# Hybrid gated-mixer trunk: v of the attentions stored as [hi, lo] side by side, two products for three, a PSUM bank per group

## The chip, the cores and the metric

The kernel runs on one core of one Trainium2 chip. The metric is the device time of one execution in microseconds, as the median of several runs of the same program. The profile is of one execution, taken by the hardware profiler, with its own time.

## The reference

Two layers run over 256 tokens of width 1024, all in f32. Each has a gated feed-forward block, a mixer with four branches, a cross-attention to 256 memory tokens and a second feed-forward block. The change is in two of the mixer's branches, the attentions (cut):

```python
y_a = conv_module(u_conv, ...)            # 31 taps, 512 channels
y_b = pool_mixer(u_pool, ...)
y_c = nsa_attention(q_n, k_c, v_c, k_s, v_s, k_w, v_w, g_nsa, ...)
y_d = banded_attention(q_s, k_s, v_s, SWA_WINDOW, swa_sinks[l])
merged = sum(gates[:, :, n] * (branches[n] @ w_branch[l, n]) for n in range(4))
x = x + rms_norm(merged @ w_out[l], mix_post_g[l])

# nsa_attention: 8 heads of 64 in 2 groups that share k and v, 256 tokens
o_c = softmax(q k_cmp) @ v_cmp            # compressed keys, 15 blocks
o_s = softmax(q k_sel) @ v_sel            # blocks of 64 chosen by o_c's scores
o_w = softmax(q k_w)  @ v_w               # band of 512
o   = g0 * o_c + g1 * o_s + g2 * o_w      # g: sigmoid gates per head
```

banded_attention is the same for the sliding window of 128 (called swa below), with one more term per head in the softmax's sum.

## The kernel before

Every f32 factor is held as a pair of reduced-precision pieces, hi (ScalarE, ACT, copies and rounds, L266) and lo = value - hi (VectorE, DVE, L269). A product is three matmuls, hi x hi, hi x lo and lo x hi (mm3), all issued from L280 on TensorE (PE). Weights come as 512 KB halves (raw) through SyncE's DMA queue (SP), are split into hi and lo, and used once. The normalised tokens are hTh and hTl, transposed.

PSUM has three pools: mm with two banks (the wide projections), acc with four (scores, values and small projections), tr with two (transposes). A bank holds 128 x 512 f32.

In an attention, the scores of two or four heads go into an acc bank, DVE and ACT make the softmax (pp), PE transposes it (L731, tr<-ident,pp), and pt_split makes pth (ACT) and ptl (DVE), 128x512 each. Then the probabilities are multiplied with v. Output rows are head dimensions, 64 for each of the two groups, columns are heads and tokens. v of group 0 has to go to rows 0 to 63 and that of group 1 to rows 64 to 127, so v is stored with zero columns: vp has, for each half of the keys (kt) and each of three kinds (NSA's selected and window v, swa's v), the columns [v0, 0, 0, v1], once for hi and once for lo. vpg takes [v0, 0] or [0, v1], and the products of both groups add up in one bank per half of the tokens (t). The zero columns are written by ACT at the setup (L404 to L412); put_v fills in v. Each product of vp is pth x hi, pth x lo and ptl x hi.

The compressed part of NSA has its probabilities in pc (DVE, two writes of 128x64 per t), transposed as tr<-ident,pc and multiplied with vc. cmp_value (L1166) adds its product to the same bank as the others and then splits the bank into y (hi by ACT, lo by DVE), which the branch's output projection reads.

nsa (L1095) and swa (L1186) are pipelines of units (t, group, pair of heads), score of one ahead of value of the one before. A scheduler sets the order of the instructions of each engine from the order in the code, from priorities (front() raises one) and from when it expects buffers to be free; the order is then fixed in the program, and each engine works its own off in turn. Beside the attentions run the conv branch's 124 taps per layer on DVE (cy<-t,sp,cy, conv_taps L949), its statistics on PE (acc<-cy,ones, conv_out L962), the projections of the mixer (mm<-hT.., in branch_chunk and gate_chunk, L868 to L896), and swa_proj (L931), which projects swa's q with 48 matmuls of 512 columns into two acc banks (acc<-hi,hTh 128x512 and its two like). The last step of the mixer is the output projection, acc<-hi,y 128x512 first.

Of the kernel before, what the change touches and what calls it, by code (L numbers as in the profile page):

```python
# [7 lines left out]
F32 = mybir.dt.float32  # L8
F32R = mybir.dt.float32r
# [3 lines left out]
ALU = mybir.AluOpType  # L13
AX = mybir.AxisListType

P = 128
# [3 lines left out]
NT = 2  # L20
# [186 lines left out]
class Trunk:  # L207
# [171 lines left out]
    def setup(self):  # L379
        nc = self.nc  # L380
        cst = self.const.tile([P, _NC - P], F32, name="cst")
        nc.sync.dma_start(cst, self.c_d[:, P:])

        def c(nm):
            a, b = _COFF[nm]
            return cst[:, a - P:b - P]

        self.c = c
        idr = self.const.tile([P, P], F32R, name="idr")
        nc.vector.tensor_copy(idr, self.ident)  # L390
        self.idr = idr
        msk = self.const.tile([P, 2, P], F32R, name="msk")
        nc.vector.tensor_copy(msk[:, 0, :], c("swal"))
        nc.vector.tensor_copy(msk[:, 1, :], c("tri"))
        self.mtri4 = msk[:, 1, None, :].to_broadcast([P, 4, P])
        self.mtri2 = msk[:, 1, None, :].to_broadcast([P, 2, P])
        self.mswa = msk[:, None, :, :].to_broadcast([P, 2, 2, P])
        self.cmneg = self.const.tile([P, 2, 16], F32R, name="cmneg")
        self.ts(self.cmneg.rearrange("p a b -> p (a b)"), c("cm"), 1.0, -NEG, ALU.subtract, ALU.mult)
        self.ones = self.const.tile([P, P], F32, name="ones")  # L400
        nc.vector.memset(self.ones, 1.0 / 512)
        self.zero = self.t4([P, 512])
        nc.vector.memset(self.zero, 0.0)
        self.vpad = []  # L404
        for i in range(2):
            row = []
            for kt in range(NT):
                v = self.const.tile([P, 3, 4, 64], F32R, name="vp%d%d" % (i, kt))
                self.act(v.rearrange("p a b c -> p (a b c)")[:, :512], self.zero)
                self.act(v.rearrange("p a b c -> p (a b c)")[:, 512:], self.zero[:, :256])  # L410
                row.append(v)
            self.vpad.append(row)  # L412
        self.vc = []
        for i in range(2):
            v = self.const.tile([P, P], F32R, name="vc%d" % i)
            self.act(v, self.zero[:, :P])
            self.vc.append(v)
        self.kc = self.const.tile([P, 2, 2, 16], F32R, name="kc")
        self.pc = self.const.tile([P, 4, P], F32, name="pc")
        nc.vector.memset(self.pc.rearrange("p a b -> p (a b)"), 0.0)  # L420
# [275 lines left out]

    def put_v(self, kind, t, ps):

        hi, lo = self.vpad[0][t][:, kind, 0::3, :], self.vpad[1][t][:, kind, 0::3, :]
        self.split(hi, lo, ps)  # L700

    def softmax(self, bank, ng, w, wgt=None, nsink=None, on_dve=False):

# [44 lines left out]
            pend = (b, r)  # L748
        pend[0](pend[1])

    def vpg(self, i, kt, kind, g):
        return self.vpad[i][kt][:, kind, 2 * g:2 * g + 2, :].rearrange("p a d -> p (a d)")

    def mixer(self, l, h):
        nc, tc = self.nc, self.tc
# [339 lines left out]
    def nsa(self, qn, kkh, kkl, gt, y, before_cmp):  # L1095
        nc = self.nc
        cm = self.c("cm").rearrange("p (t c) -> p t c", t=2)
        out = [None, None]

        def score(t, g, pr):  # L1100
            h0 = g * 4 + pr * 2
# [19 lines left out]
            return ps  # L1121

        def value(t, g, pr, ps):
            first = out[t] is None
            if first:
                out[t] = self.pacc((P, 4, P))
            dst = out[t][:, 2 * pr:2 * pr + 2, :]
            if t == 0:
                p = self.pt_split([ps[j][:, br, :] for br in range(2) for j in range(2)])
                for br in range(2):  # L1130
                    self.pv(dst, p, slice(2 * br, 2 * br + 2), self.vpg(0, 0, br, g), self.vpg(1, 0, br, g),
                            first and br == 0, False)
                return
            for br in range(2):
                p = self.pt_split([ps[j][:, br, kt * P:(kt + 1) * P] for kt in range(2) for j in range(2)])
                for kt in range(2):
                    self.pv(dst, p, slice(2 * kt, 2 * kt + 2), self.vpg(0, kt, br, g), self.vpg(1, kt, br, g),
                            first and br == 0 and kt == 0, False)

        def cmp_score(t):  # L1140
            if t == 0:
# [24 lines left out]
        def cmp_value(t, _):  # L1166
            tok = slice(t * P, (t + 1) * P)
            p = self.pt_split([self.pc[:, r, :] for r in range(4)])
            self.pv(out[t], p, slice(0, 4), self.vc[0], self.vc[1], False, True)
            self.split(y[0][:, :, tok], y[1][:, :, tok], out[t])  # L1170

        units = [(t, g, pr) for t in range(NT) for g in range(2) for pr in range(2)]
        ready = {}
        for i, u in enumerate(units):
            ready[u] = score(*u)
            if i == 4:
                cmp_score(0)
            if i:
                value(*units[i - 1], ready[units[i - 1]])
            if i == 6:  # L1180
                cmp_value(0, None)
        cmp_score(1)
        value(*units[-1], ready[units[-1]])
        cmp_value(1, None)

    def swa(self, qs, kks, y, mp):  # L1186
        ns = mp.tile([P, 8], F32, name="ns")
        self.ts(ns, self.S_("sinks"), -1.0)
        out = [None, None]

        def score(t, g, pr):
            if t == 0:
                bank = self.pacc((P, 4, P))
                self.matmul(bank, self.idr, self.mtri4, True, False)
                for r in range(4):
                    q = qs[0][:, g * 4 + r, :]
                    self.matmul(bank[:, r, :], q, kks[:, g, 0:P], False, False)
                    self.matmul(bank[:, r, :], q, kks[:, 2 + g, 0:P], False, True)
                return self.softmax(bank, 4, P, None, ns[:, g * 4:g * 4 + 4], True)
            h0 = g * 4 + pr * 2  # L1200
            bank = self.pacc((P, 2, S))
            self.matmul(bank.rearrange("p a (b k) -> p a b k", b=2), self.idr, self.mswa, True, False)
            for j in range(2):
                q = qs[1][:, h0 + j, :]
                self.matmul(bank[:, j, :], q, kks[:, g, :], False, False)
                self.matmul(bank[:, j, :], q, kks[:, 2 + g, :], False, True)
            return self.softmax(bank, 2, S, None, ns[:, h0:h0 + 2], True)

        def value(t, g, pr, p):
            first = out[t] is None  # L1210
            if first:
                out[t] = self.pacc((P, 4, P))
            if t == 0:
                p = self.pt_split([p[:, r, :] for r in range(4)])
                self.pv(out[0], p, slice(0, 4), self.vpg(0, 0, 2, g), self.vpg(1, 0, 2, g), first, g == 1)
            else:
                dst = out[1][:, 2 * pr:2 * pr + 2, :]
                p = self.pt_split([p[:, j, kt * P:(kt + 1) * P] for kt in range(2) for j in range(2)])
                for kt in range(2):
                    self.pv(dst, p, slice(2 * kt, 2 * kt + 2), self.vpg(0, kt, 2, g), self.vpg(1, kt, 2, g),  # L1220
                            first and kt == 0, kt == 1)
            if g == 1 and (t == 0 or pr == 1):
                tok = slice(t * P, (t + 1) * P)
                self.split(y[0][:, :, tok], y[1][:, :, tok], out[t])

        self.pipeline([(lambda t=t, g=g, pr=pr: score(t, g, pr), lambda p, t=t, g=g, pr=pr: value(t, g, pr, p))
                       for t in range(NT) for g in range(2) for pr in range(1 + t)])

# [134 lines left out]
```

## Time and profile before

| | us |
|---|---|
| median of 3 runs | 1590.31 (1589.11 to 1591.09) |
| profiled execution | 1588.27 |
| its span in the trace | 1586.5 |
| PE busy | 1561.8 |
| DVE busy | 1148.1 |
| ACT busy | 860.8 |
| granted clock of PE, mean | 0.999 |

The page gives busy time per engine over the span. PE's matmuls overlap, so the sum of the durations is more than the span they take, and their start-to-start distance is what one costs. 285.57 MB come in by DMA at 180 GB/s on average. The rows of the trace give the start of an instruction from the span's start, its duration, engine, line, operation, and output and inputs with their shape. A row with x2 or x4 holds that many matmuls.

### The profile page before, as it was taken

The page shows a single profiled execution, that of the slowest core. Times are in us where ns is not written, and L with a number is a line of the kernel's source. Part 1 is how long each engine was busy: PE and PEld are TensorE (multiplying, and loading weights), DVE is VectorE, ACT ScalarE, POOL GpSimd, SP SyncE. Part 2 cuts the span into 40 slices and gives each one's busy share as a digit, 9 for nine tenths or more (in the row PEclk, how much of TensorE's full clock was granted, in tenths as well). Part 3 has the DMA queues.
Part 4 walks back from the last instruction along what each step waited for, and adds up shares of the span by engine and source line. Part 5 has one row for each costly group of instructions (what it writes and reads, how often), then busy time and mean ns, then how long its engine had stood idle before and what let it go on. Part 6 is the DMA issues. An engine that isn't in the chain of part 4 may idle for free.

```text
span 1586.5 us, 28413 instructions
## 1 busy us (share of the span) xinstructions
PE 1561.8 (98%) x11324; PEld 1468.4 (93%) x11324; DVE 1148.1 (72%) x1875; ACT 860.8 (54%) x1461; POOL 21.6 (1%) x44
## 2 busy tenths in 40 slices
PE   6999999999999999999999999999999999999998
PEld 6999889999998988999899987999999999899986
DVE  6666579999878576666566656799998785676653
ACT  6445455675656464545444544656755564554442
POOL 0000000000000000000000000000000000000000
PEclk9999999999999999999999999999999999999999
DMA  7555646644455554555655566465435565445562
GB/s 256 179 188 179 231 152 208 214 134 133 154 173 196 187 184 152 180 191 177 230 172 190 189 198 208 143 227 177 146 121 167 176 206 183 160 164 187 188 201 99
DMA packets 79909, 285.57 MB, mean 180 GB/s; under 512 B 8992, under 2 KB 9760, under 8 KB 79776
## 3 DMA queue, kind: packets, MB, share of 16 engines
q1 hardware_dynamic: 79776, 283.75, 54.0%
q8 instruction: 89, 1.46, 0.4%
q14 instruction: 44, 0.36, 0.1%
HBM read 282.67 MB, written 1.05 MB: 179 GB/s over the span
## 4 chain that ended last, share of the span: by engine, by line
PE 89%; DMA 4%; DVE 3%; ACT 2%; issue 1%; SPq 0%; DVEq 0%; POOLq 0%; ACTq 0%
PE mm L280 55%; PE acc L280 32%; DMA raw<-in_stream_dram 3%; ACT hi L266 1%; DVE lo L269 1%; PE tr L474 1%; PE tr L731 1%; DMA x<-in_x_dram 1%; DVE cy L277 0%; PE tr L280 0%; ACT yw L266 0%; DVE yw L269 0%; PE tr L693 0%; ACT t L266 0%; PE tr L632 0%
## 5 line engine op out<-in xcount | busy, mean ns | idle before, releaser
L269 DVE TENSOR_TENSOR lo<-raw,hi 128x1024 fp32r<-128x1024 f32 (+1 forms) x468 | 565.8, 1215 | 259.6 <-ACT hi L266 255.2
L266 ACT ACTIVATE hi<-raw 128x1024 fp32r<-128x1024 f32 (+1 forms) x468 | 489.6, 1054 | 347.6 <-PE mm L280 211.0
L280 PE MATMUL mm<-hTh,lo 128*128 128x256 f32 x2048 | 575.2, 281 | 0.0
L280 PE MATMUL mm<-hTl,hi 128*128 128x256 f32 x2048 | 573.8, 280 | 0.0
L280 PE MATMUL mm<-hTh,hi 128*128 128x256 f32 x2048 | 573.1, 280 | 0.5 <-ACT hi L266 0.5
L280 PEld LDWEIGHTS mm<-hTh,hi 128*128 128x128 f32 x2048 | 385.1, 188 | 1.1 <-ACT hi L266 0.9
L280 PEld LDWEIGHTS mm<-hTh,lo 128*128 128x128 f32 x2048 | 384.9, 188 | 0.6
L280 PEld LDWEIGHTS mm<-hTl,hi 128*128 128x128 f32 x2048 | 384.9, 188 | 0.3
L280 PE MATMUL acc<-hi,mid 128*128 128x512 f32 x512 | 156.9, 390 | 0.5 <-ACT hi L266 0.5
L280 PEld LDWEIGHTS acc<-hi,mid 128*128 128x128 f32 x512 | 96.0, 188 | 21.3 <-ACT hi L266 1.6
L277 DVE SCALAR_TENSOR_TENSOR cy<-t,sp,cy 128x256 f32<-128x256 f32 x240 | 107.9, 480 | 0.0
L266 ACT ACTIVATE mid<-t 128x256 fp32r<-128x256 f32 x76 | 31.8, 419 | 137.4 <-DVE t L277 137.4
L280 PE MATMUL acc<-lo,mid 128*128 128x512 f32 x256 | 98.0, 390 | 0.1
L280 PE MATMUL mm<-y,hi 128*128 128x256 f32 x512 | 94.1, 282 | 0.0
L280 PE MATMUL acc<-hi,hTh 128*128 128x256 f32 (+2 forms) x272 | 87.6, 323 | 1.5 <-ACT hTh L266 1.4
L280 PE MATMUL acc<-hi,hTl 128*128 128x256 f32 (+2 forms) x272 | 87.6, 322 | 1.2 <-DVE hTl L269 1.2
L280 PE MATMUL acc<-lo,hTh 128*128 128x256 f32 (+2 forms) x272 | 87.4, 322 | 0.0
L280 PEld LDWEIGHTS mm<-y,hi 128*128 128x128 f32 x512 | 79.5, 188 | 1.0
L280 PE MATMUL mm<-y,lo 128*128 128x256 f32 x256 | 72.6, 284 | 0.0
L277 DVE SCALAR_TENSOR_TENSOR t<-t,mm 128x256 f32<-128x256 f32 x160 | 66.8, 417 | 2.6
L269 DVE TENSOR_TENSOR mid<-t,mid 128x256 fp32r<-128x256 f32 x76 | 32.4, 426 | 36.9 <-ACT mid L266 36.9
L280 PEld LDWEIGHTS acc<-lo,mid 128*128 128x128 f32 x256 | 48.1, 188 | 10.8 <-DVE lo L269 1.0
(248 smaller groups left out, 2240.1 us busy)
## 6 DMA issues: line engine op xcount, KB each, us to landing
raw<-in_stream_dram SPq DMA_DIRECT2D x508, 512.0 KB, 4.4
g<-in_gains_dram SPq DMA_DIRECT2D x18, 512.0 KB, 3.8
raw<-in_stream_dram SPq DMA_DIRECT2D x8, 280.0 KB, 3.2
t<-in_mem_dram SPq DMA_DIRECT2D x4, 512.0 KB, 4.0
out_dram<-x SPq DMA_DIRECT2D x4, 256.0 KB, 2.0
x<-in_x_dram SPq DMA_DIRECT2D x2, 256.0 KB, 3.1
x<-in_x_dram SPq DMA_DIRECT2D x1, 512.0 KB, 9.3
t<-in_small_dram SPq DMA_DIRECT2D x2, 256.0 KB, 5.2
```

Source lines behind the costliest of these rows:

```text
L266: return self.nc.scalar.activation(out, in_, func, **kw)
L269: return self.nc.vector.tensor_tensor(out, a, b, op=op)
L277: return self.nc.vector.scalar_tensor_tensor(out, a, s, b, op0=op0, op1=op1)
L280: return self.nc.tensor.matmul(out, lhsT, rhs, start=start, stop=stop, skip_group_check=True)
L474: tr = self.nc.tensor.transpose(pt[:, j, :], xn[:, j * P:(j + 1) * P], self.ident)
L731: self.nc.tensor.transpose(pt[:, j, :], s_, self.ident)
```

## The change

v is stored once per half of the keys, without zeros, as [hi0, lo0, lo1, hi1] of 64 columns each for the two groups (vhl). vpg takes [hi0, lo0] or [lo1, hi1]. pv2 then multiplies that with pth and with ptl, two matmuls in place of three; the output rows are now one group's product with hi in one half and with lo in the other. (The product of ptl with lo, which mm3 leaves out, comes with it.) So the two groups no longer share a bank: each (t, group) gets a bank of acc. fold brings the halves together when a group is done: ACT copies the half with lo from the bank to yf in SBUF, shifted to the group's rows, and DVE adds the half with hi, 64x512 each, both with a raised priority. NSA's compressed product goes to an acc bank of its own, and DVE adds it to yf, 128x512. y is split from yf. In all, a layer has eight folds. The eight zero writes of the setup are gone. The compressed product itself still has three matmuls. The scheduler sets the order of all instructions anew.

```diff
-        self.vpad = []
-        for i in range(2):
-            row = []
-            for kt in range(NT):
-                v = self.const.tile([P, 3, 4, 64], F32R, name="vp%d%d" % (i, kt))
-                self.act(v.rearrange("p a b c -> p (a b c)")[:, :512], self.zero)
-                self.act(v.rearrange("p a b c -> p (a b c)")[:, 512:], self.zero[:, :256])
-                row.append(v)
-            self.vpad.append(row)
+        self.vhl = [self.const.tile([P, 3, 4, 64], F32R, name="vp%d" % kt) for kt in range(NT)]
...
-        hi, lo = self.vpad[0][t][:, kind, 0::3, :], self.vpad[1][t][:, kind, 0::3, :]
-        self.split(hi, lo, ps)
+        self.split(self.vhl[t][:, kind, 0::3, :], self.vhl[t][:, kind, 1:3, :], ps)
...
+    def vpg(self, kt, kind, g):
+        return self.vhl[kt][:, kind, 2 * g:2 * g + 2, :].rearrange("p a d -> p (a d)")
+    def pv2(self, out, p, n, v, start, stop):
+        self.matmul(out, v, p[0][:, n, :], start, False)
+        self.matmul(out, v, p[1][:, n, :], False, stop)
+    def fold(self, yf, bank, g):
+        a, b = slice(g * 64, g * 64 + 64), slice(64 - g * 64, 128 - g * 64)
+        with self.front():
+            self.act(yf[a], bank[b])
+            self.tt(yf[a], yf[a], bank[a], ALU.add)
...
         def value(t, g, pr, ps):                      # nsa
-            first = out[t] is None
+            first = pr == 0
             if first:
-                out[t] = self.pacc((P, 4, P))
-            dst = out[t][:, 2 * pr:2 * pr + 2, :]
+                bank[0] = self.pacc((P, 4, P))
+                if g == 0:
+                    out[t] = self.ap.tile([P, 4, P], F32, tag="yf", bufs=2, name="yf")
+            dst = bank[0][:, 2 * pr:2 * pr + 2, :]
...
+            if pr == 1:
+                self.fold(out[t], bank[0], g)
...
         def cmp_value(t, _):
...
-            self.pv(out[t], p, slice(0, 4), self.vc[0], self.vc[1], False, True)
-            self.split(y[0][:, :, tok], y[1][:, :, tok], out[t])
+            cmp = self.pacc((P, 4, P))
+            self.pv(cmp, p, slice(0, 4), self.vc[0], self.vc[1], True, True)
+            with self.front():
+                self.tt(out[t], out[t], cmp, ALU.add)
+                self.split(y[0][:, :, tok], y[1][:, :, tok], out[t])
```

swa's value is changed in the same way as nsa's.

The first place is PE at the end of NSA in layer 1. In the order of before, the 48 projection matmuls for swa's q (hi, lo with hTh, hTl, 128x512) stand between the products of the probabilities (pth, ptl with vp and vc) and the transposes of pp:

```order
L280 MATMUL acc<-hi,hTh 128x512
L280 MATMUL acc<-lo,hTh 128x512
L280 MATMUL acc<-hi,hTl 128x512
L280 MATMUL acc<-hi,hTh 128x512
L280 MATMUL acc<-lo,hTh 128x512
L280 MATMUL acc<-hi,hTl 128x512
L280 MATMUL acc<-pth,vc_214 128x512
L280 MATMUL acc<-pth,vp_202 128x256
L280 MATMUL acc<-ptl,vc_214 128x512
L280 MATMUL acc<-pth,vc_216 128x512
L731 MATMUL tr<-ident,pp 128x128 x4
L280 MATMUL acc<-ptl,vp_202 128x256
```

In the order of after the same stretch has transposes and products alone, and the projection begins behind the last compressed product and four conv statistics:

```order
L280 MATMUL acc<-ptl,vp_202 128x256
L280 MATMUL acc<-pth,vp_203 128x256
L280 MATMUL acc<-ptl,vp_203 128x256
L280 MATMUL acc<-pth,vp_202 128x256
L722 MATMUL tr<-ident,pc 128x128 x4
L280 MATMUL acc<-ptl,vp_202 128x256
L280 MATMUL acc<-pth,vp_203 128x256
L280 MATMUL acc<-ptl,vp_203 128x256
L280 MATMUL acc<-pth,vc_204 128x512
L280 MATMUL acc<-cy,ones 128x256 x4
L280 MATMUL acc<-hi,hTh 128x512
L280 MATMUL acc<-lo,hTh 128x512
```

All 48 projection matmuls moved from ahead of the last tr<-ident,pc to behind it, and three of the conv statistics with them.

The second place is DVE at the same end of NSA, around its last write of pc (s_.. are columns of softmax sums and gates, t_.. the compressed scores, cy the conv taps). In the order of before:

```order
L269 TENSOR_TENSOR ptl<-tr,pth 128x512
L277 SCALAR_TENSOR_TENSOR cy<-t_2789,sp,cy 128x256 x2
L269 TENSOR_TENSOR s_3762<-s_3762,gt_2618 128x8
L269 TENSOR_TENSOR lo<-raw,hi 128x1024
L277 SCALAR_TENSOR_TENSOR cy<-t_2789,sp,cy 128x256
L269 TENSOR_TENSOR pc<-t_3759,s_3762 128x4x16 x2
L269 TENSOR_TENSOR lo<-raw,hi 128x1024
L277 SCALAR_TENSOR_TENSOR cy<-t_2789,sp,cy 128x256
L269 TENSOR_TENSOR lo<-raw,hi 128x1024 x2
L269 TENSOR_TENSOR ptl<-tr,pth 128x512
```

In the order of after:

```order
L269 TENSOR_TENSOR t_3741<-t_3741,cst 128x128
L1163 TENSOR_REDUCE s_3743<-t_3741 128x8
L273 TENSOR_SCALAR s_3743<-s_3743 128x8
L1165 RECIPROCAL s_3744<-s_3743 128x8
L269 TENSOR_TENSOR s_3744<-s_3744,gt_2608 128x8
L269 TENSOR_TENSOR pc<-t_3741,s_3744 128x4x16 x2
L269 TENSOR_TENSOR ptl<-tr,pth 128x512 x3
L269 TENSOR_TENSOR yf<-yf,acc 64x512
L269 TENSOR_TENSOR cy<-cy,acc 128x1024
L269 TENSOR_TENSOR yf<-yf,acc 128x512
L269 TENSOR_TENSOR y<-yf,y 128x4x128
L269 TENSOR_TENSOR lo<-raw,hi 128x1024 x2
```

Before, a weight split (lo) and taps stand just ahead of pc and splits behind it. After, the last ptl's and the yf adds stand right behind pc, and no tap or split stands in the rows ahead of it.

## Rows read from the trace of the kernel before

**Rows 1.** The page: busy us (share) per engine.
```profile
PE 1561.8 (98%) x11324; PEld 1468.4 (93%) x11324; DVE 1148.1 (72%) x1875; ACT 860.8 (54%) x1461; POOL 21.6 (1%) x44
```

**Rows 2.** Timeline of PE (start, us, instruction) and groups of 371.4 to 390.
```profile
371.25 0.28 PE L280 MATMUL mm<-hTh,lo 128*128 128x256 f32 x1
371.37 0.59 PE L280 MATMUL acc<-cy,ones 128*128 128x256 f32 x2
...
372.03 0.40 PE L280 MATMUL acc<-lo,hTh 128*128 128x512 f32 x1
372.26 0.39 PE L280 MATMUL acc<-hi,hTl 128*128 128x512 f32 x1
...
L280 PE MATMUL acc<-hi,hTh 128*128 128x512 f32 x16 | 6.6, 413 | 0.0
```

**Rows 3.** Windows: busy us of PE, PEld, DVE, ACT, POOL; clock, DMA share, GB/s.
```profile
237.00:290.00 53.00, 51.37 (x434) 50.62 (x433) 50.81 (x108) 30.56 (x47) 0.00 (x0) 1.00 0.65 214
290.00:340.00 50.00, 49.77 (x413) 48.77 (x412) 49.41 (x111) 34.70 (x91) 0.00 (x0) 1.00 0.53 175
340.00:386.00 46.00, 46.00 (x338) 43.31 (x337) 42.78 (x101) 29.08 (x61) 0.00 (x0) 1.00 0.35 117
```

**Rows 4.** Timeline of PE and DVE about the last pc, and PE's output projection.
```profile
385.41 0.36 DVE L269 TENSOR_TENSOR pc<-t,s 128x64 f32<-128x64 f32 x2
...
388.52 0.60 PE L280 MATMUL acc<-cy,ones 128*128 128x256 f32 x2
388.95 0.60 PE L731 MATMUL tr<-ident,pc 128*128 128x128 f32 x4
...
479.56 0.86 PE L280 MATMUL acc<-hi,y 128*128 128x512 f32 x3
```

**Rows 5.** Groups of the whole span, shapes apart: products of probabilities with v.
```profile
L280 PE MATMUL acc<-pth,vp 128*128 128x256 f32 x128 | 28.8, 285 | 0.0
...
L280 PE MATMUL acc<-ptl,vp 128*128 128x256 f32 x64 | 18.3, 286 | 0.2
```

**Rows 6.** DVE groups of 237 to 386 (busy, mean ns, idle before); two timeline rows.
```profile
L269 DVE TENSOR_TENSOR lo<-raw,hi 128x1024 fp32r<-128x1024 f32 x48 | 58.4, 1220 | 2.5 <-ACT hi L266 2.5
...
L269 DVE TENSOR_TENSOR ptl<-tr,pth 128x512 fp32r<-128x512 f32 x12 | 8.1, 678 | 1.6 <-ACT pth L266 1.6
...
381.72 0.68 DVE L269 TENSOR_TENSOR ptl<-tr,pth 128x512 fp32r<-128x512 f32 x1
382.32 0.19 DVE L1159 RECIPROCAL s<-s 128x8 f32<-128x8 f32 x1
```

**Rows 7.** Groups, shapes apart: the nearest DVE and ACT instructions to the new ones.
```profile
L269 DVE TENSOR_TENSOR t<-t,sp 64x240 f32<-64x240 f32 x8 | 4.3, 575 | 1.2 <-ACT t L266 1.2
...
L269 DVE TENSOR_TENSOR y<-acc,y 128x512 fp32r<-128x512 f32 x8 | 5.5, 690 | 3.6 <-ACT y L266 3.6
...
L266 ACT ACTIVATE y<-acc 128x512 fp32r<-128x512 f32 x8 | 4.7, 591 | 10.6 <-PE acc L280 10.6
...
L269 DVE TENSOR_TENSOR vp<-acc,vp 128x128 fp32r<-128x128 f32 x12 | 3.2, 282 | 0.1
```

**Rows 8.** The start: ACT and PE timeline; the load of x from the chain.
```profile
2.01 3.41 ACT L266 ACTIVATE vp<-t 128x512 fp32r<-128x512 f32 x8
...
3.52 9.29 DMA x<-in_x_dram
...
14.10 0.58 PE L280 MATMUL acc<-hi,hTh 128*128 128x256 f32 x1 [1.37 <-ACT hTh L266]
...
17.77 0.41 PE L280 MATMUL acc<-hi,hTh 128*128 128x256 f32 x1
17.98 0.32 PE L280 MATMUL acc<-lo,hTh 128*128 128x256 f32 x1
```

**Rows 9.** Timeline of PE in layer 2, the same two matmuls.
```profile
1170.61 0.60 PE L731 MATMUL tr<-ident,pc 128*128 128x128 f32 x4
...
1261.15 0.86 PE L280 MATMUL acc<-hi,y 128*128 128x512 f32 x3
```

More of the change, by code (lines that the diff above doesn't have):

```diff
@@ L749, in pipeline @@
         pend[0](pend[1])
-    def vpg(self, i, kt, kind, g):
-        return self.vpad[i][kt][:, kind, 2 * g:2 * g + 2, :].rearrange("p a d -> p (a d)")
+    def vpg(self, kt, kind, g):
[8 more added lines that the diff above has]
+            self.tt(yf[a], yf[a], bank[a], ALU.add)
     def mixer(self, l, h):
@@ L1097, in nsa @@
         cm = self.c("cm").rearrange("p (t c) -> p t c", t=2)
-        out = [None, None]
+        out, bank = [None, None], [None]
         def score(t, g, pr):
@@ L1130, in value @@
                 for br in range(2):
[L1131 to L1138, printed above, removed]
+                    self.pv2(dst, p, slice(2 * br, 2 * br + 2), self.vpg(0, br, g), first and br == 0, br == 1)
+            else:
+                for br in range(2):
+                    p = self.pt_split([ps[j][:, br, kt * P:(kt + 1) * P] for kt in range(2) for j in range(2)])
+                    for kt in range(2):
+                        self.pv2(dst, p, slice(2 * kt, 2 * kt + 2), self.vpg(kt, br, g),
+                                 first and br == 0 and kt == 0, br == 1 and kt == 1)
+            if pr == 1:
+                self.fold(out[t], bank[0], g)
         def cmp_score(t):
@@ L1188, in swa @@
         self.ts(ns, self.S_("sinks"), -1.0)
-        out = [None, None]
+        out, bank = [None, None], [None]
         def score(t, g, pr):
@@ L1209, in value @@
         def value(t, g, pr, p):
-            first = out[t] is None
-            if first:
-                out[t] = self.pacc((P, 4, P))
+            if pr == 0:
+                bank[0] = self.pacc((P, 4, P))
+                if g == 0:
+                    out[t] = mp.tile([P, 4, P], F32, tag="yf", bufs=2, name="yf")
             if t == 0:
                 p = self.pt_split([p[:, r, :] for r in range(4)])
-                self.pv(out[0], p, slice(0, 4), self.vpg(0, 0, 2, g), self.vpg(1, 0, 2, g), first, g == 1)
+                self.pv2(bank[0], p, slice(0, 4), self.vpg(0, 2, g), True, True)
             else:
-                dst = out[1][:, 2 * pr:2 * pr + 2, :]
+                dst = bank[0][:, 2 * pr:2 * pr + 2, :]
                 p = self.pt_split([p[:, j, kt * P:(kt + 1) * P] for kt in range(2) for j in range(2)])
                 for kt in range(2):
[L1220 to L1224, printed above, removed]
+                    self.pv2(dst, p, slice(2 * kt, 2 * kt + 2), self.vpg(kt, 2, g), pr == 0 and kt == 0, kt == 1)
+            if t == 0 or pr == 1:
+                self.fold(out[t], bank[0], g)
+                if g == 1:
+                    tok = slice(t * P, (t + 1) * P)
+                    self.split(y[0][:, :, tok], y[1][:, :, tok], out[t])
         self.pipeline([(lambda t=t, g=g, pr=pr: score(t, g, pr), lambda p, t=t, g=g, pr=pr: value(t, g, pr, p))
```

## The prediction

> **What bounds the kernel now.** I read the busy times of the page first, then the stretch that the change touches, by windows and by timelines. TensorE (PE) is busy for 1561.8 of 1586.5 us, 98% [rows 1]. So nearly every matmul stands in the end time at its start-to-start pace, not at the longer duration that a row shows, because matmuls overlap: 0.12 us for 256 columns, 0.23 us for 512, 0.43 us for a conv statistic (cy against ones) or four transposes [rows 2, 4]. The first look therefore says that fewer matmuls give a shorter kernel.
>
> The second look goes to the stretch. The attention over NSA's heads lies at 237 to about 390 us in layer 1, and there VectorE (DVE) is nearly as full as PE: 50.81 of 53, 49.41 of 50 and 42.78 of 46 us, 6.0 us idle in 149 [rows 3]. It works off splits of weights, 58.4 us of them [rows 6], and conv taps between the attention's own steps. At the end of the stretch PE stays full, 46.00 of 46 [rows 3], only because it has something else to do: from about 372 on it runs 48 matmuls of 512 columns that project q for the sliding-window attention (acc from hi and lo weights and hT), 48 x 0.23 = 10.9 us, in between the attention's tail [rows 2] (there is the row of one of the three kinds, 16 each). They need nothing from DVE and hold two of the four acc banks. Behind them come the last transposes of the compressed probabilities (pc) at 388.95, for which DVE wrote pc at 385.41, and from there to the first matmul of the output projection, at 479.56, PE runs without a break: 90.6 us [rows 4]. Layer 2 has the same distance, 1170.61 to 1261.15 [rows 9].
>
> **Removed.** Each product of probabilities with v has two matmuls in place of three: in both layers together 192 of 256 columns become 128 [rows 5], and by the order 12 of 512 become 8. 64 x 0.117 + 4 x 0.23 = 8.4 us, 4.2 a layer, of which 2.8 lie in NSA and 1.4 in the sliding-window attention.
>
> At the start ACT's eight zero writes go, 3.41 us from 2.01 [rows 8]. ACT is free at 5.42 in before, but a piece of x that the chain waits for lands only at 3.52 + 9.29 = 12.81 [rows 8]. That DMA hides most of it; what may be left is the work that ACT does behind 5.42 for the first pieces of x. I put it between 0 and 2 us and take -0.5, near the hidden end, since the load was issued long before ACT was free and lands 7 us after.
>
> **Added off PE.** Per layer: eight ACT copies and eight DVE adds of 64x512 (fold), and two DVE adds of 128x512 for the compressed part. The nearest DVE row is 128x512 out of PSUM, 0.69 us long [rows 7], and 0.60 from start to start for one of that size [rows 6]. Half the partitions should save nothing where the time goes by columns, but no row of before has 64x512. The only row on 64 partitions is 64x240 at 0.575, which would make 1.2 us of 512 columns; the smallest PSUM row, 128x128 at 0.282, is the other end [rows 7]. I take 0.60, from the row with the same columns. ACT's copies are like y from acc, 0.591 [rows 7], and ACT has room (29.08 of 46 [rows 3]), so they cost nothing but delay. Of the DVE adds four stand ahead of the last pc in the order of after; one tap more stands there too (0.39), one weight split less (1.13), one ptl less (0.60). Sum on DVE up to pc: 2.4 + 0.39 - 1.13 - 0.60 = +1.0 us.
>
> **Moved, and this decides.** A bank per (t, group) in place of one per t, and one more for the compressed part, means that scores, two value banks and the compressed sum can hold all four acc banks in NSA's tail. In the order of after the 48 projection matmuls no longer stand in the tail; all of them come after the last pc transposes. PE then has only the tail's own work, about 9 us of transposes and products, for a stretch that DVE sets, and cannot reach ahead. What DVE sets hardly moves, so the 10.9 us of filler that were free in before become time behind the meeting point.
>
> Worked out from the last pc transposes to the first matmul of the output projection: +48 x 0.227 = 10.9 for the projection; three more conv statistics behind the point, 3 x 0.43 = 1.3; eleven products of 256 and two of 512 fewer, -1.3 and -0.45. 90.6 + 10.45 = 101.0 us, as long as PE is full there, which the rows of before show (it had no gap in 90.6 us, and DVE has the most to do early in it).
>
> When do the transposes start? By the count on DVE, pc is written at 385.41 + 1.0 = 386.4 if the 6.0 us idle up to there stay. In PE's order four products stand ahead of the transposes whose ptl DVE makes right behind pc, so the transposes come 0.36 + 0.68 and a few products later, about 388.1: 0.85 earlier than 388.95, since no projection stands in PE's queue any more. The last rows of DVE before pc are the attention's own chain alone, with no tap or split; if what DVE waited for there comes sooner, because PE is free, pc may be ready at 384.1, and the point 3 us earlier. That second value is my estimate from the durations of the chain's steps. I take 1.65 earlier, nearer the count. Per layer: 10.45 - 1.65 = +8.8 us. Two layers have the same order: 17.6 - 0.5 at the start = **+17 us**. The 8.4 us removed are in this sum where they can show: of NSA's 2.8 a layer most lie ahead of the point, in PE time that now waits for DVE anyway, and are worth nothing there.
>
> The profiled execution has 1588.27 us (span 1586.5, 1.8 around it), so 1605.3 by this; the median is 1590.31, 2.0 above the profiled one, which gives **1607**. For the ends: with all of DVE's idle time gone (6 us earlier, less its 1.0 of new work), 5.45 a layer, minus 2 at the start, +8.9; with adds at 0.3 us another 1.2 a layer less, which ends at 1596.8. With adds at 1.2 us DVE is 2.4 later a layer, and with no idle time regained 10.45 + 1.0 + 2.4 = 13.9, times two: 1618.
>
> **Rivals.** A: the order, as above. B, on the other side: the saved matmuls count at face value, -8.4 - 0.5, so 1581 to 1582. For it: PE's 98% [rows 1]. Against it: the point from which it decides. The pc transposes must start at 388.95 - 10.45 = 378.5 for a layer to lose nothing, and 4.2 us before that for face value. So pc must be ready 8 to 12 us before 386.4, while DVE had 6.0 us idle up to there, and its idle time is put to ACT's hi and pth, 2.5 and 1.6 [rows 6], not to matmuls that go away. It holds only if DVE's order of after brings pc forward past taps and splits by more than I counted.
>
> C: the clock. At the start, after PE had been idle, matmuls of 256 columns begin 0.21 apart up to 17.98 [rows 8], later 0.12 apart [rows 2], where the granted clock reads 1.00 [rows 3]: the lower and the upper of the levels 1.2 and 2.4 GHz. In before the tail has no gap. In after PE waits some 8 us of the tail in pieces of a few us. If the clock falls there and has to climb as at the start (17 matmuls from 14.10 to 17.98, each 0.095 too long), that is 1.6 us a layer, +3.2: 1610. The pieces are short and matmuls stand between them, so I hold it for the less likely.
>
> The Trainium skill, "TensorE: Matmul & The Clock Gate", section "Why this matters for your kernels", wants no idle gaps between matmul bursts, because a clock that has fallen must climb again. By that rule, rival C holds in both layers; no gap of before's tail shows it.
>
> D: half of B. pc comes forward by 8 to 9 us a layer, the moved projection is paid for, and nothing is left of the gain: 1587 to 1593. A bank that comes free early on the chip cannot bring it about, since each engine works its instructions off in the order printed above. That the products aren't removed can be left out: the order has 68 matmuls fewer.
>
> **How the numbers follow.** A has 0.70, C 0.18 (inside A's range, above its middle), B 0.08, D 0.04. The likeliest is A: 1607. The range 1596 to 1618 holds A with its unknown prices and C; B and D, 0.12 together, stay out. Faster by over 0.2% (3.2 us, about what a measurement of this kernel can tell from no change) is B, 0.08; within it D, 0.04; slower A and C, 0.88.
>
> **What would show it.** In after, in layer 1: the last projection tile of the mixer before the tail ends near 364, and from there to the pc transposes PE is idle for some 8 to 16 us, with DVE near full up to its last taps. From the pc transposes to the first output-projection matmul it is about 101 us, in both layers. The yf adds last about 0.7, the copies 0.6 or less. The granted clock in the tail tells A from C. I am wrong if PE stays above 95% in the tail, or if that distance is 90 us, or if the pc transposes come before 380.

## The result and the profile after

The changed kernel takes 1608.24 us (median of 4, 1607.96 to 1608.85) against 1589.73 us for the kernel before, run beside it on the same chip: a ratio of 1.0121, 95% interval 1.0108 to 1.0133, or 18.5 us slower by the medians (19.2 by the ratio). The forecast was 1607, with 1596 to 1618 as its range.

The page of the changed kernel, with the same columns as [rows 1], shows nothing at first sight: PE is as busy as before, with 68 matmuls fewer.

```profile
PE 1568.9 (98%) x11256; PEld 1469.8 (92%) x11256; DVE 1162.0 (72%) x1895; ACT 866.8 (54%) x1469; POOL 21.5 (1%) x44
```

The windows of the stretch do (start:end and length, then busy us of PE, PEld, DVE, ACT and POOL, granted clock, DMA share, GB/s). Up to 364 us PE is as full as in [rows 3]. Then comes NSA's tail:

```profile
340.00:364.00 24.00, 23.79 (x197) 23.21 (x195) 23.91 (x54) 16.44 (x34) 0.00 (x0) 1.00 0.47 152
364.00:386.00 22.00, 15.45 (x71) 12.53 (x72) 19.40 (x55) 14.04 (x39) 0.00 (x0) 0.72 0.14 48
...
368.00:377.00 9.00, 6.99 (x25) 5.94 (x26) 9.00 (x28) 4.10 (x11) 0.00 (x0) 0.50 0.09 34
377.00:383.00 6.00, 4.43 (x30) 3.38 (x28) 5.27 (x19) 5.34 (x17) 0.00 (x0) 1.00 0.01 3
383.00:389.00 6.00, 5.46 (x22) 4.68 (x23) 2.80 (x6) 1.77 (x4) 0.00 (x0) 0.72 0.00 0
```

From 364 to 386 us PE is busy 15.45 of 22 us and works part of that at the lower clock level: 0.50 from 368 to 377 is 1.2 of 2.4 GHz. It goes back to 1.00 and falls once more. Shorter windows put the first fall between 366 and 367, and show PE busy without a break ahead of the rise:

```profile
365.00:366.00 1.00, 0.71 (x6) 0.62 (x6) 1.00 (x3) 1.00 (x5) 0.00 (x0) 1.00 0.66 242
366.00:367.00 1.00, 0.23 (x3) 0.00 (x0) 1.00 (x5) 1.00 (x6) 0.00 (x0) 0.85 0.69 234
367.00:368.00 1.00, 0.58 (x1) 0.29 (x1) 1.00 (x3) 1.00 (x5) 0.00 (x0) 0.50 0.72 246
372.00:377.00 5.00, 5.00 (x18) 4.21 (x19) 5.00 (x12) 1.29 (x4) 0.00 (x0) 0.51 0.00 0
```

The weight stream stands still behind it (48 GB/s, then nothing). PE's timeline (start, us, instruction, idle before and what ended it) shows what it waits for:

```profile
363.52 0.27 PE L722 MATMUL tr<-ident,pp 128*128 128x128 f32 x1
365.29 0.94 PE L722 MATMUL tr<-ident,pp 128*128 128x128 f32 x6 [1.50 <-ACT pp L266]
367.09 0.58 PE L280 MATMUL acc<-pth,vp 128*128 128x256 f32 x1 [0.85 <-ACT pth L266]
368.12 0.58 PE L280 MATMUL acc<-ptl,vp 128*128 128x256 f32 x1 [0.45 <-DVE ptl L269]
...
371.87 1.08 PE L722 MATMUL tr<-ident,pc 128*128 128x128 f32 x4 [1.89 <-DVE pc L269]
...
374.23 0.41 PE L280 MATMUL acc<-msk,idr 128*128 128x256 f32 x1
...
375.30 0.41 PE L280 MATMUL acc<-msk,idr 128*128 128x256 f32 x1
...
384.90 1.05 PE L722 MATMUL tr<-ident,pc 128*128 128x128 f32 x4
...
388.75 0.58 PE L280 MATMUL acc<-hi,hTh 128*128 128x512 f32 x1
...
487.74 1.09 PE L280 MATMUL acc<-hi,y 128*128 128x512 f32 x4
```

Every step of the attention's chain is there bare: softmax (pp), transposes, pth, ptl, products, and no other matmul in between. The two scores of the last unit (acc<-msk,idr begins a score) come only at 374.23 and 375.30. In the kernel before they came at 353.50 and 359.92, with the last pc transposes at 388.95 [rows 4]:

```profile
353.50 0.29 PE L280 MATMUL acc<-msk,idr 128*128 128x256 f32 x1
...
359.92 0.28 PE L280 MATMUL acc<-msk,idr 128*128 128x256 f32 x1
```

In the changed kernel, at 388.75 the projection begins, behind everything, and at 487.74 the output projection. Layer 2 is the same (1176.61 and 1279.38).

### The profile page after: what moved, and what is told of

It reads as the page before. It is cut to its first block, busy times and chain, and to the rows that moved or that the text cites. A ratio compares the mean times of both kernels' runs of the same rounds, so it can differ in the third digit from the quotient of the medians.

```text
span 1606.1 us, 28314 instructions
## 1 busy us (share of the span) xinstructions
PE 1568.9 (98%) x11256; PEld 1469.8 (92%) x11256; DVE 1162.0 (72%) x1895; ACT 866.8 (54%) x1469; POOL 21.5 (1%) x44
## 4 chain that ended last, share of the span: by engine, by line
PE 87%; DMA 4%; DVE 3%; ACT 3%; issue 1%; SPq 0%; POOL 0%; DVEq 0%; POOLq 0%; ACTq 0%
PE mm L280 52%; PE acc L280 33%; DMA raw<-in_stream_dram 4%; ACT hi L266 1%; DVE lo L269 1%; PE tr L722 1%; PE tr L466 1%; DVE cy L277 1%; DMA t<-in_mem_dram 1%; ACT pp L266 0%; PE tr L280 0%; ACT yw L266 0%; ACT t L266 0%; PE tr L685 0%; DVE ptl L269 0%
## 5 line engine op out<-in xcount | busy, mean ns | idle before, releaser
L280 PEld LDWEIGHTS acc<-hi,hTl 128*128 128x128 f32 x272 | 52.3, 192 | 6.2 <-DVE hTl L269 2.8
```

The costliest lines, as they stand in the source:

```text
L280: return self.nc.tensor.matmul(out, lhsT, rhs, start=start, stop=stop, skip_group_check=True)
```

## The experiments

The comparisons below are all with the kernel before on the same chip. In the table, layer 1 is cut at three points: the first matmul of the pool branch's gate projection (236.01 in before), the last pc transposes, and the output projection's first matmul.

| kernel | median, us | ratio (95%) | first cut | cut 1 to pc | pc to output projection |
|---|---|---|---|---|---|
| before | 1587.9 to 1589.7 | 1 | 236.01 | 152.94 | 90.61 |
| changed | 1608.24 | 1.0121 (1.0108, 1.0133) | 234.10 | 150.80 | 102.84 |
| own bank alone | 1614.59 | 1.0158 (1.0139, 1.0177) | 235.95 | 152.93 | 102.65 |
| two products alone | 1584.24 | 0.9971 (0.9959, 0.9984) | 236.21 | 151.79 | 89.40 |
| NSA alone | 1610.30 | 1.0137 (1.0119, 1.0155) | 233.12 | 150.54 | 103.02 |
| sliding window alone | 1596.29 | 1.0045 (1.0030, 1.0059) | 235.36 | 152.96 | 94.92 |
| the same, no folds | 1585.95 | 0.9983 (0.9973, 0.9993) | 234.29 | 152.60 | 89.12 |
| the same, direct | 1595.04 | 1.0043 (1.0030, 1.0055) | 235.53 | 152.64 | 94.20 |
| changed, q in mm | 1611.28 | 1.0136 (1.0117, 1.0154) | 233.85 | 158.02 | 95.88 |
| before, q in mm | 1597.81 | 1.0058 (1.0044, 1.0072) | 235.88 | 156.78 | 90.46 |
| changed, two in tr | 1619.72 | 1.0196 (1.0180, 1.0211) | 233.28 | 163.26 | 95.58 |
| the same, direct | 1612.92 | 1.0153 (1.0137, 1.0170) | 234.47 | 164.03 | 96.87 |

**The bank alone.** The compressed product gets its own bank in the kernel before, with an ACT copy and a DVE add of 128x512 to join it:

```diff
-            self.pv(out[t], p, slice(0, 4), self.vc[0], self.vc[1], False, True)
+            cmp = self.pacc((P, 4, P))
+            self.pv(cmp, p, slice(0, 4), self.vc[0], self.vc[1], True, True)
+            self.act(yf, out[t]); self.tt(yf, yf, cmp, ALU.add)   # then y from yf
```

> The kernel before with three products per value and padded v, but with the compressed product of NSA in an acc bank of its own: ACT copies the value bank to SBUF and DVE adds the compressed bank, one each of 128x512 per half of the tokens. Nothing is saved on TensorE, no fold is added. In its order all 48 projection matmuls stand behind the last pc transposes, as in the changed kernel, with 100.3 us of matmul work from there to the output projection where before has 88.8. Theory (bank and order): +9 to +10 us a layer as in the changed kernel (10.2 measured there), 1607 to 1611. Rival (the folds' own work on DVE and ACT is what costs): nearly nothing of the folds is here, so within 3 us of before.

It is 25.1 us slower by its ratio, more than the theory said and far from the rival. Its timeline of PE has the picture of the changed kernel, without any of its folds or its two-product form:

```profile
373.62 0.28 PE L280 MATMUL acc<-msk,idr 128*128 128x256 f32 x1
374.20 0.28 PE L280 MATMUL acc<-msk,idr 128*128 128x256 f32 x1
377.82 0.39 PE L280 MATMUL acc<-cmneg,idr 128*128 128x256 f32 x1 [0.53 <-ACT pp L266]
382.48 0.88 PE L731 MATMUL tr<-ident,pp 128*128 128x128 f32 x2 [2.79 <-ACT pp L266]
383.86 1.54 PE L731 MATMUL tr<-ident,pp 128*128 128x128 f32 x6 [0.51 <-ACT pp L266]
386.36 0.58 PE L280 MATMUL acc<-ptl,vp 128*128 128x256 f32 x1 [0.32 <-DVE ptl L269]
388.87 0.57 PE L731 MATMUL tr<-ident,pc 128*128 128x128 f32 x3
...
491.52 0.86 PE L280 MATMUL acc<-hi,y 128*128 128x512 f32 x3
```

The last scores come 14 to 20 us later than in before, and the last pc transposes at the same time (152.93 after the first cut, 152.94 before). So one more acc bank held, with a copy and an add per half of the tokens, is enough for the whole damage: the scores don't run ahead, the projection doesn't come in, PE stands, and what it could have done waits behind pc. The same copy and add without the bank wasn't run, so the bank's share is not told apart from theirs and from the new order that the scheduler makes for any edit.

**NSA alone, sliding window alone.** In each run one attention has the change and the other its form of before.

```diff
# NSA alone: v of kinds 0 and 1 as [hi0, lo0, lo1, hi1], pv2, fold and cmp bank in nsa; swa as before
# sliding window alone: kind 2 so, pv2 and fold in swa; nsa as before, one yf buffer
```

> The change in NSA alone; the sliding-window attention keeps its padded v and three products. Its order has all 48 projection matmuls behind the last pc transposes. Theory (order): the whole loss of the changed kernel stays and the 2.8 us saved in the sliding-window attention are missing, so 18.5 + 2.8, 1608 to 1612. Rival (the loss is spread over both attentions by their folds): about half of the changed kernel's loss, 1598 to 1600.

> The change in the sliding-window attention alone; NSA and its banks as before. In its order the projection stays in NSA's tail. Theory (order): 8 products of 256 and 2 of 512 columns fewer a layer, 1.4 us each, so -2.8, and about -1 at the start for zero writes that fall away: 1585 to 1588. Rival (folds cost): four folds a layer stay, so slower than before by 3 us or more.

NSA alone is 21.8 us slower by its ratio, as expected: the whole loss is there. The sliding window alone was expected to gain and loses 7.1, so there the rival held. PE's timeline, ACT's copy of the last half and the DVE add, all of layer 1:

```profile
472.82 1.31 PE L280 MATMUL mm<-y,hi 128*128 128x256 f32 x3 [3.75 <-ACT y L266]
...
469.33 0.59 ACT L266 ACTIVATE yf<-acc 64x512 f32<-64x512 f32 x1
...
471.42 0.69 DVE L269 TENSOR_TENSOR yf<-yf,acc 64x512 f32<-64x512 f32 x1
```

PE waits 3.75 us for y at the end of this attention, where in before the first such matmul came at 470.16 without a wait, and the clock falls (0.81 from 468 to 477). The row of before:

```profile
470.16 0.40 PE L280 MATMUL mm<-y,hi 128*128 128x256 f32 x2
```

**Without folds, and with a shorter chain.** Twice more the sliding window alone. First y comes right from each bank's half with hi:

```diff
-                self.fold(out[t], bank[0], g)
-                if g == 1: self.split(y[0][:, :, tok], y[1][:, :, tok], out[t])
+                self.split(y[0][a, :, tok], y[1][a, :, tok], bank[0][a])
```

> The change in the sliding-window attention alone, without folds: y is split right from each bank's half with hi, 64x512, so the half with lo is left out of the result. Same matmuls as in the run with the change in this attention alone, which was 7.4 us slower than before with a stall of 4 us of TensorE at the end of this attention, a layer. If the folds cause that stall (copy, add, then split, two more steps ahead of the branch's first matmul), it goes, and the saved matmuls show: -2.8 and -0.7 at the start, 1585 to 1587. If the stall comes from the new order of the matmuls, it stays: 1593 to 1597.

It gains 2.7 by its ratio, and pc to output projection is 1.49 us shorter, as the 1.4 saved in this attention predict. In the direct form y hi is copied at once, and only y lo takes in the other half:

```diff
+                    self.act(y[0][a, :, tok], bank[0][a])
+                    self.act(yf[a], bank[0][b])
+                    self.tt(yf[a], yf[a], y[0][a, :, tok], ALU.subtract)
+                    self.tt(y[1][a, :, tok], yf[a], bank[0][a], ALU.add)
```

> The change in the sliding-window attention alone, with y hi copied right from the bank's half and the half with lo added to y lo; the result is complete. Theory: as without folds (-3.2 us measured there): 1584 to 1587.5, a version ahead of both kernels. Rival (two more DVE and ACT instructions per group, whatever they wait for, cost as the folds did): 1592 or more.

That missed: 6.8 slower. The chain from the last product to y hi is as short as in before, and still the branch waits. The last products themselves come late, at 468.08, where without folds they come at 463.24 (1.3 us of that is there already at the pc transposes). From 455 to 468 PE has no wait. It has done the other projections by the last products, where without folds it has 3.4 us of matmuls left between them and y. Then it waits 1.29 us for y from ACT, 0.85 for a gate and 0.47 for DVE's y. That the units are later because the folds' instructions stand in the queues of ACT and DVE among the softmax, pth and ptl is a reading of the order; no run here shows it.

**The projection moved back.** swa's q projection goes to the two mm banks, in the changed kernel and, as a control, in the kernel before:

```diff
-        acc = self.tok_major("qs", h, 512)
+        acc = self.tok_major("qs", h, 512, 2, self.pmm)
```

> The changed kernel with one edit: the projection of the sliding-window q writes to the two mm banks in place of two acc banks, so NSA's banks can't keep it out. In its order all 48 projection matmuls stand in NSA's tail again, ahead of the last pc transposes; from there to the output projection are 88.3 us of matmul work (changed kernel 99.2). Theory (bank and order): the tail is filled, the clock stays up, and the loss of 10 to 12 us a layer is gone: 1582 to 1590. Rival (folds and the longer chain cost in themselves): at least half of the loss stays, 1598 or more.

> The kernel before with the same edit, the projection into the mm banks; all else as before. Control for the last one. Theory: TensorE had no idle time in the tail of the kernel before, so there is nothing to gain from a free bank: within 4 us of before, 1586 to 1593. If acc banks were short in the kernel before as well, it gains 4 us or more.

Both missed, and the first has the time of its rival. The projection is back in the tail of the changed kernel, from 363.56 to 375.65, and pc to output projection shrinks from 102.84 to 95.88. But the last pc transposes come 7.2 us later. PE fills the tail with the projection and then waits for the same bare chain, which starts later:

```profile
363.56 0.40 PE L280 MATMUL mm<-hi,hTh 128*128 128x512 f32 x1
375.65 0.39 PE L280 MATMUL mm<-hi,hTl 128*128 128x512 f32 x1
...
379.57 0.28 PE L280 MATMUL acc<-msk,idr 128*128 128x256 f32 x1
...
387.54 2.54 PE L722 MATMUL tr<-ident,pp 128*128 128x128 f32 x8 [2.24 <-ACT pp L266]
```

The last unit's scores begin at 379.57 now, 5.3 us later than in the changed kernel. So to put the displaced projection back does not take the loss away. What this leaves is the reading that the scores have to run ahead, which the next runs try, and the rival, the folds' own cost, which has the bank alone against it: that kernel has none of the folds and loses more. The control is 9.2 us slower than before, with pc 3.8 us later, so this edit is not free itself; against it the change costs 13.5 us (1611.28 to 1597.81).

**Two banks from tr.** The compressed scores and product go to the tr pool, which leaves acc to scores and values:

```diff
-        sc = self.pacc((P, 8, 2, 16))
+        sc = self.ptr((P, 8, 2, 16))
-            cmp = self.pacc((P, 4, P))
+            cmp = self.ptr((P, 4, P))
```

> The changed kernel with two banks of acc relieved: NSA's compressed scores and its compressed product go to the two tr banks. In its order the last NSA score has 20.4 us of matmul work ahead of the last pc transposes (28.6 before, 4.8 in the changed kernel, 4.8 with the projection in the mm banks, 6.1 with the compressed product in its own acc bank), and all 48 projection matmuls are in the tail. Theory as it stands after the last runs: late scores are what empties the tail, because the chain from score to pc is then bare; with banks for them the 10 us a layer go, and what may stay is the longer chain at the end of the sliding-window attention, 0 to 4 us a layer: 1581 to 1592. Rival (the folds' work on DVE and ACT sets the end of NSA): 1600 or more.

> The last kernel, and in the sliding-window attention no fold ahead of the split: y hi is copied from the bank's half right away, and the half with lo is added to y lo, so that the branch's first matmul waits for one ACT copy. Theory: the longer chain at the end of this attention costs nothing then, 8.4 us of matmuls saved and about 1 at the start: 1579 to 1586. Rival: it stays with the last one within 2 us, if no wait was there.

Both missed by 25 us and more, and the first has the time of its rival; it is the slowest kernel of all. The second is 6.8 us faster than the first, so its rival missed as well. The first one's PE timeline, and its windows:

```profile
363.70 0.36 PE L280 MATMUL acc<-msk,idr 128*128 128x256 f32 x1
...
367.34 0.39 PE L280 MATMUL acc<-ptl,vp 128*128 128x256 f32 x1 [1.42 <-DVE ptl L269]
372.29 1.09 PE L722 MATMUL tr<-ident,pc 128*128 128x128 f32 x4 [3.66 <-DVE s L709]
...
384.51 0.29 PE L280 MATMUL tr<-cmneg,idr 128*128 128x256 f32 x1
...
396.54 0.60 PE L722 MATMUL tr<-ident,pc 128*128 128x128 f32 x4
...
364.00:376.00 12.00, 4.52 (x17) 2.68 (x16) 12.00 (x37) 8.48 (x24) 0.00 (x0) 0.74 0.26 87
376.00:386.00 10.00, 10.00 (x51) 8.45 (x51) 4.98 (x8) 3.77 (x7) 0.00 (x0) 0.80 0.01 2
386.00:397.00 11.00, 11.00 (x60) 9.29 (x60) 9.27 (x21) 6.28 (x9) 0.00 (x0) 1.00 0.28 96
```

The last head score is early again, at 363.70, and yet the loss stays, so early scores of the heads are not enough. PE stands from 364 to 376 (busy 4.52 of 12 us, DVE all 12) and is full from there to the last pc transposes at 396.54. The compressed scores (tr<-cmneg) come at 384.51, behind a part of the projection, where they stood at 377.82 with the own bank alone and at 378.01 in the changed kernel. The transposes of pp and pc now share two tr banks with the compressed scores and product. That it is the tr banks that hold the compressed scores back is read from what moved, and wasn't tried apart.

**The start.** The zero writes leave ACT's setup in two ways: to GpSimd, and to the start of the first mixer.

```diff
-                self.act(v...[:, :512], self.zero)
+                nc.gpsimd.tensor_copy(v...[:, :512], self.zero)      # first run
+        if l == 0: ... self.act(vf[:, :512], z)                      # second run, in _mixer
```

> The kernel before with its eight zero writes on GpSimd instead of ACT; the rest and the order from the first layer on as before. If the start of the changed kernel is earlier because ACT is free of them (its matmuls run 2.0 us ahead from 38 us on), this gains about 2 us: 1587 to 1588.5. If something else sets the start, no difference within 0.5 us.

> The kernel before with ACT's eight zero writes moved from the setup to the start of the first mixer, so that ACT and the order of DVE at the start are as in the changed kernel; nothing else is changed. If the 2.0 us that the changed kernel gains by 38 us are the zero writes, with DVE's first norm ahead of the cast of ident, this gains 1.5 to 2.5 us: 1586 to 1588. If the new order of the start without the rest gives nothing, no difference within 0.7 us.

The first run missed on the wrong side: 7.6 us slower by its ratio. The order on DVE changed with the move: four weight splits, which wait for ACT's hi and that for its DMA, now stand ahead of x's norm, which runs at 17.38 (9.96 in before, ahead of all splits), and PE's first matmul comes at 18.18 instead of 10.76.

```profile
10.92 2.45 DVE L269 TENSOR_TENSOR lo<-raw,hi 128x1024 fp32r<-128x1024 f32 x2 [2.54 <-ACT hi L266]
14.68 1.23 DVE L269 TENSOR_TENSOR lo<-raw,hi 128x1024 fp32r<-128x1024 f32 x1 [1.31 <-ACT hi L266]
...
17.38 1.41 DVE L277 SCALAR_TENSOR_TENSOR t<-x,s,g 128x512 f32<-128x512 f32 x2
```

The second run is equal to before (1.0004, 0.9995 to 1.0013), as the second case of its expectation had it, but its trace has the gain: the first acc<-hi,mid matmul of the first feed-forward block, at 143.11 in before, starts 2.4 us earlier, at 140.71. That is given back at the first mixer, where the writes now take ACT's time ahead of hT.

```profile
209.65 3.42 ACT L266 ACTIVATE vp<-t 128x512 fp32r<-128x512 f32 x8 [2.84 <-DVE t L774]
```

So the start is worth about 2 us if the writes go away, as in the changed kernel.

**The removed matmuls alone.** The kernel before without its third product of v, with the banks, v and zero writes of before:

```diff
+    def pv2(self, out, p, n, vh, vl, start, stop):
+        self.matmul(out, vh, ph, start, False)
+        self.matmul(out, vh, pl, False, stop)
```

> The kernel before with the third product of v left out (probabilities hi against v lo): 68 matmuls fewer, as in the changed kernel, with the padded v, the banks and the zero writes of before and no fold; so v lo is left out of the result. Its order keeps the last NSA score 25.0 us of matmul work ahead of the last pc transposes (28.6 before) and the projection in the tail, all but 3. Theory (bank and folds are the whole loss): the saved matmuls count in full, -8.4 less at most 2 where VectorE sets the end of NSA: 1579 to 1583. Rival (VectorE sets NSA's end in any case, so matmuls saved ahead of it are worth nothing): only the 2.8 us behind it count, 1585 to 1587.

It gains 4.6 us by its ratio (2.5 to 6.5), so of 8.4 us about half show, between the two forecasts and nearer to the rival. The profiled execution, the slowest of the six, is only 1.8 us shorter than before's. In it pc to output projection is shorter by 1.21 and 1.19 us in the two layers, where 1.4 each were saved, and cut 1 to pc is shorter by 1.15 in one and longer by 0.70 in the other, where 2.8 each were saved. So the matmuls saved behind pc count; those ahead of it show little, as far as one trace tells.

## Why the prediction was right, step by step

The ledger of the two profiled executions, whose spans are 19.6 us apart, by the cuts of the table:

| step | predicted | measured |
|---|---|---|
| start, up to the first cut | -0.5 | -1.9 |
| first cut to pc transposes, layers 1 and 2 | -1.65 each | -2.1, -1.4 |
| pc transposes to output projection | +10.45 each | +12.2, +12.2 |
| all else | 0 | +0.6 |

The mechanism was right for the changed kernel: the time of pc hardly moves, PE loses what it did beside it, and that stands behind the pc transposes. Both times are near the forecast, pc to output projection 102.84 for 101.0. That the total is as near is in part luck, errors of opposite sign: the start gave 1.4 us more than forecast, and the two distances cost 3.5 us more. What the prediction took for granted besides, that the projection is free in the tail, did not hold when it was tried: with q in mm it is back there, and pc comes 7.2 us later.

The terms that were off. The **start** was put near the hidden end and is worth 2; the argument that x's DMA hides the writes failed, since with ACT free the chain at the start no longer runs over x at all but over the first weights. The **distance** is 1.8 us longer than the count. From 384.90 to 388.75 PE takes 3.85 us for four transposes, three products of 256 columns, one of 512 and four statistics, 2.7 us at the pace of [rows 2, 4]. And at the end of the sliding-window attention it waits for y:

```profile
478.12 0.36 PE L280 MATMUL mm<-y,hi 128*128 128x256 f32 x1
479.23 0.39 PE L280 MATMUL mm<-y,hi 128*128 128x256 f32 x1 [0.74 <-DVE y L269]
```

That is about 1.1 and 1.0 us: the slower clock and a wait at the folds, the two things that the sum had left at zero.

**Rival C** was given 0.18 and its condition came true: the clock does fall in the tail, twice. The prediction named the granted clock as what tells A from C, so by its own sign C happened and not A, the likeliest; the sizes don't tell them apart, with 1608.24 measured between 1607 and 1610. C was held for less likely since the waits would be short. They are: PE had waited 1.50 us and was in the wait of 0.85 us when the clock fell. The waits of 0.45 and 1.89 us came when it was down already. PE's idle time, 6.55 us from 364 to the last pc transposes, is also less than the 8 to 16 that were to show A: PE is busy 14.35 us there, for work that the prediction put at about 9, since part of it runs at the lower clock. C's price was about right (1.6 a layer expected, 1.1 behind pc as just counted). What the slow matmuls ahead of pc cost can't be told apart from the waits there. The Trainium skill, "TensorE: Matmul & The Clock Gate", section "Why this matters for your kernels", warns of idle gaps between matmul bursts. The trace agrees that such gaps bring the clock down, to 0.50 here, but the gaps ahead of the fall are shorter than those that the page speaks of.

**Rival B** was 0.08, and its price was too high besides: with no bank and no fold in the way, the removed matmuls give 4.6 us and not 8.4. What the prediction said of the changed kernel, that NSA's saved matmuls lie ahead of the point and are worth little, fits the trace of that run too.

**The folds** were costed at +1.0 us up to pc and nothing at the end of the sliding-window attention. DVE's add and ACT's copy are as estimated; groups of the whole span:

```profile
L269 DVE TENSOR_TENSOR yf<-yf,acc 64x512 f32<-64x512 f32 x16 | 10.9, 682 | 3.0 <-ACT yf L266 2.8
L266 ACT ACTIVATE yf<-acc 64x512 f32<-64x512 f32 x16 | 9.5, 593 | 2.8 <-PE acc L280 2.5
```

What they do at the end of the sliding window was missed: alone they turn a gain of 2.7 into a loss of 7.1. In the whole change that cost does not show, only the wait of about 1 us. Whether it is the extra 12 us between the two attentions that give ACT and DVE time to catch up wasn't tried, and stays open. So does the question that matters for using the change: whether any division of the eight banks allows a bank per group without the loss. The two tried, q in mm and the compressed part in tr, did not. Nor is it DVE alone that sets the time of pc. The chain that the profile follows back in the changed kernel (start, us, engine, tile, line) goes through DVE, then through ACT for pp, then through DVE's short compressed steps to pc:

```profile
364.39 1.23 DVE lo L269
...
376.28 0.61 DVE s L698
...
376.91 0.96 ACT pp L266 x4
...
378.93 1.82 ACT pp L266 x6
...
382.79 0.36 DVE pc L269 x2
```

Of DVE's part, 364.39 to 376.89, conv taps take 6.3 us and a fold's add 0.59. So the adds weigh little on that chain and the taps more. Whether pc comes sooner with the taps out of the way wasn't tried.

No version here that computes everything is ahead of the kernel before.

## What to carry to other kernels

When a change takes one more buffer in a pool that is already full, find what used the last free one, before counting the instructions saved: here it was scores that ran 29 us ahead of the last pc transposes, and one bank less cost 25 us with only a copy and an add beside it. Look for the point where the engine meets the result of another, and count first what was saved behind it; what was saved ahead of it showed little here. And to put displaced work back where it was need not be a cure: here the rest of the order was another by then, and the loss stayed.

## What the hardware showed beside

A DVE add on 64 partitions takes as long as on 128: 682 ns for 64x512 with a bank as input, 690 for 128x512 out of a bank [rows 7]; ACT's copy 593 against 591. PE's granted clock fell to 0.50 between 366 and 368, behind a wait of 1.50 us, six transposes and a part of a wait of 0.85 us. It was back at 1.00 at 377, behind 5 us in which PE was busy without a break, and stayed there to 383 with PE busy 4.43 of 6 us.
